# Combining the attention groups inside the attention stage, with five weight slots instead of seven

## The chip, the core and the metric

The kernel runs on one core of a Trainium2 chip as a single program. The metric is the device time of one execution in microseconds (us). TensorE is called PE in the profile, VectorE DVE, ScalarE ACT, GpSimd POOL, and SP is the engine that issues most DMA transfers. PEld is PE's loading of the stationary operand, which overlaps with its matmuls.

## The reference

One step of a hybrid decoder layer over 2048 prompt tokens (and eight sample tokens, which ride along) with a model width of 1024. One wide input projection feeds everything. Three attention groups with different dilations share eight head slots, and per position the groups of a slot are averaged with weights from their softmax denominators; a gate multiplies the average. Beside it runs an HGRN2 recurrence with eight heads. Cut to what matters here:

```
GROUPS = ((128, 1), (512, 4), (2048, 16))          # (window, dilation)
h = rms_norm(x, norm_w)
for g, (win, dil) in enumerate(GROUPS):
    q, k, v = three 512-wide column groups of h @ w_in
    o[g], lse[g] = dilated_attn_prompt(q, k, v, win, dil, slopes[g])
mix = softmax(stack(lse), axis=0)                  # over the three groups
att = einsum('gnth,gnthe->nthe', mix, stack(o))
att = att * silu(h @ w_in[:, attention gate])
hq, fl, hi, hgate = four 1024-wide column groups of h @ w_in
ho, s_new = hgrn2_chunked(silu(hq) * dk**-0.5, ...)
ho = rms_norm(ho, hg_norm_w) * silu(hgate)
merged = sigmoid(ga) * (att @ w_att_proj) + sigmoid(gb) * (ho @ w_hg_proj)
y = x + merged @ w_out
```

## The kernel before

The tokens are worked off in two halves of 1024 (p = 0 and p = 1). For each half the program goes through `att_stage(p)`, `cb_stage(p)` and `hg_stage(p)`, in that order, with the natural-layout projections and the merges between and behind them. In the profiled execution the first half's three stages lie at about 262 to 706, 706 to 816 and 816 to 1245 us, those of the second half at 1600 to 2085, 2085 to 2180 and 2180 to 2550 us.

Projections. `t_pair` projects h onto two 128-wide groups of columns of w_in at once, by a scheme of seven products in place of eight. The seven operands on the token side are A11, S1, S2, A12, S3, S4, A22 (sums of quarters of h, made once); the seven on the weight side are W0 to W6, made by `w_combos` from four loaded quarters (`wr`). Each operand is split into a high part and a low part, hh/hl for tokens and wh/wl for weights, so that three matmuls (L413 hh with wh, L415 hl with wh, L416 hh with wl) over four slices of the contraction, 12 in all, make one product. The weight split is one ScalarE instruction (L193, writes wh) and one VectorE instruction that needs its result (L194, writes wl). The products go into three PSUM banks pa, pb and pc; intermediate sums are copied to `cc` by ScalarE (L420), and results leave through evacuation functions (VectorE L456 adds a cc). In the first half a pair is done in two passes, one of 256 and one of 260 columns, so each of the seven weights is used twice; in the second half one pass of 512 uses each once. The number of wh/wl buffers is the first argument of `open_T`, the number of wr buffers the second.

Attention. For each of four slots j and three groups g, `att_proj` projects q and k with one pair, and `att_side` of the (j, g) before it computes scores (L568 and L585), exponentials (L590), transposes of the probabilities (L600) and the weighted sums (L614), and stores the result with its denominators to `natt[g][j]`. The side matmuls go between those of the pair.

Combination. `att_gates(j)` is a pair that makes the gates of slots j and j+1 and stores them to `gs_scr`. `combine(j, cs)` loads, for each block c of 512 tokens, the three groups' results into `na` and averages them on VectorE (L672 to L688, with one exponential on ScalarE, L676); `combine_T` transposes the average (L696), multiplies it by the gate and stores it. `merge_pair` makes the merge gates (its bank is read by the ScalarE sigmoid L707). All of it stands in `cb_stage`.

HGRN. `hg_stage` does eight heads, each with a pair for gates and, shared by neighbours, pairs for f and q; the chain of a head (L912 to L967 and a normalization, L938 to L993) runs on the side, from `kn`, the copy of the transposed keys, on (L925).

The order on each engine is set by a scheduler from the order of the code and priorities, and is fixed in the program: an instruction waits for those ahead of it on its engine, and its buffers for their last readers.

Of the kernel before, what the change touches and what calls it, by code (L numbers as in the profile page):

```python
# [10 lines left out]
F32 = mybir.dt.float32  # L11
# [7 lines left out]
P = 128  # L19
# [57 lines left out]
def body(ctx, tc, x_p, x_s, c128, c512, c2048, st_in, norm_w, w_in, w_ap, w_hp, w_out, hg_nw, lbl, fin_w,  # L77
# [7 lines left out]
    sto = nc.sync.dma_start  # L85
# [5 lines left out]
    def pool(name, bufs=1, space=None):  # L91
        if space == DRAM:
            return tc.tile_pool(name=name, bufs=bufs, space=space)
        kw = {} if space is None else {"space": space}
        return tc.tile_pool(name=name, bufs=bufs, reuse_waits="tile", **kw)
# [46 lines left out]
    def ps_side():  # L142
        return cur["x"].tile([P, 512], F32, name="px", tag="px")
# [242 lines left out]
    def open_T(slots, raws):  # L386
        tp["st"] = ExitStack()
        tp["p"] = tp["st"].enter_context(pool("wt"))
        tp["n"] = slots, raws
# [57 lines left out]
    def put(dst, ps, add, view=lambda x: x):  # L447
        if add is None:
            A.copy(out=dst, in_=view(ps))
        else:  # L450
            V.tensor_tensor(out=dst, in0=view(ps), in1=view(add), op=ALU.add)

    def val(ps, add):
        if add is None:
            return ps
        V.tensor_tensor(out=add, in0=ps, in1=add, op=ALU.add)  # L456
        return add

    def att_proj(at, p, j, g):
        dil = GROUPS[g][1]  # L460
        qT = at.tile([P, HALF], F32, name="qT", tag="qT", bufs=2)
        kT = at.tile([P, HALF * (1 + p)], F32, name="kT", tag="kT", bufs=2)
        q4 = qT.rearrange("p (b r i) -> p b r i", b=2, r=4)
        q16 = qT.rearrange("p (r i) -> p r i", r=16)
        k4 = kT.rearrange("p (b r i) -> p b r i", r=4, i=P)
        k16 = kT.rearrange("p (h r i) -> p h r i", r=16, i=64)
        if p == 1:
            n = (128, 512, 1024)[g]
            dma(kT[:, 0:n], kscr[g][j])

        def evac(is_k):
            def f(r, off, npr, ps, add):
                t0 = r * 512 + off
                if dil == 1:
                    s0 = t0 + (P if is_k and p else 0)
                    put((kT if is_k else qT)[:, s0:s0 + npr], ps, add)
                elif dil == 4:
                    i0, ni = off // 4, npr // 4
                    o = k4[:, r + p] if is_k else q4[:, r]
                    put(o[:, :, i0:i0 + ni], ps, add, lambda x: x.rearrange("p (i r) -> p r i", r=4))  # L480
                else:
                    i0, ni = t0 // 16, npr // 16
                    o = k16[:, p] if is_k else q16
                    put(o[:, :, i0:i0 + ni], ps, add, lambda x: x.rearrange("p (i r) -> p r i", r=16))
            return f

        c0 = g * 1536 + j * P
        t_pair(p, (c0, c0 + AW), (g * 8 + j, g * 8 + 4 + j), (evac(False), evac(True)))
        if p == 0:
            sto(kscr[g][j], (kT[:, HALF - P:HALF], kT[:, 512:1024], kT)[g])  # L490
        return qT, kT
# [156 lines left out]
            if n < 6:  # L648
                a, b = na, score(n + 3)

    def att_gates(pl, p, j, sto=sto):
        def evac(j):
            def f(r, off, npr, ps, add):
                z = val(ps, add)
                gt = pl.tile([P, 512], F32, name="gm", tag="gm", bufs=3)[:, 0:npr]
                A.activation(out=gt, in_=z, func=AF.Sigmoid)
                V.tensor_tensor(out=gt, in0=z, in1=gt, op=ALU.mult)
                t0 = p * HALF + r * 512 + off
                sto(gs_scr[j][:, t0:t0 + npr], gt)
            return f  # L660

        t_pair(p, (OFF_G + j * P, OFF_G + (j + 1) * P), (48 + j, 49 + j), (evac(j), evac(j + 1)))

    def combine(cb, j, cs):
        pend = []
        for c in cs:
            na = cb.tile([P, 3, 4, 132], F32, name="na", tag="na", bufs=4)
            for g in range(3):
                dma(na[:, g], natt[g][j][c * 512:(c + 1) * 512].rearrange("(i u) c -> i u c", u=4))
            mx = cb.tile([P, 4, 2], F32, name="mx", tag="mx", bufs=2)  # L670
            w3 = cb.tile([P, 3, 4, 2], F32, name="w3", tag="w3", bufs=2)
            V.tensor_tensor(out=mx, in0=na[:, 0, :, 128:130], in1=na[:, 1, :, 128:130], op=ALU.min)  # L672
            V.tensor_tensor(out=mx, in0=mx, in1=na[:, 2, :, 128:130], op=ALU.min)
            for g in range(3):
                V.tensor_tensor(out=w3[:, g], in0=mx, in1=na[:, g, :, 128:130], op=ALU.subtract)
            A.activation(out=w3, in_=w3, func=AF.Exp)  # L676
            wd = cb.tile([P, 3, 4, 2], F32, name="wd", tag="wd", bufs=2)
            V.tensor_tensor(out=wd, in0=w3, in1=na[:, :, :, 130:132], op=ALU.mult)
            V.tensor_tensor(out=mx, in0=wd[:, 0], in1=wd[:, 1], op=ALU.add)
            V.tensor_tensor(out=mx, in0=mx, in1=wd[:, 2], op=ALU.add)  # L680
            V.reciprocal(out=mx, in_=mx)
            for g in range(3):
                V.tensor_tensor(out=w3[:, g], in0=w3[:, g], in1=mx, op=ALU.mult)
                nv = na[:, g, :, 0:128].rearrange("p u (h e) -> p u h e", h=2)
                V.tensor_tensor(out=nv, in0=nv, in1=w3[:, g].unsqueeze(3).to_broadcast([P, 4, 2, E]), op=ALU.mult)
            nv = na[:, 0, :, 0:128]
            V.tensor_tensor(out=nv, in0=nv, in1=na[:, 1, :, 0:128], op=ALU.add)
            V.tensor_tensor(out=nv, in0=nv, in1=na[:, 2, :, 0:128], op=ALU.add)  # L688
            pend.append((c, na))
        return j, pend  # L690

    def combine_T(cb, j, pend):
        for c, na in pend:
            pt = ps_side()
            for u in range(4):
                TE.transpose(pt[:, u * P:(u + 1) * P], na[:, 0, u, 0:128], ident)  # L696
            gt = cb.tile([P, 512], F32, name="gc", tag="gm", bufs=3)
            dma(gt, gs_scr[j][:, c * 512:(c + 1) * 512])
            V.tensor_tensor(out=gt.rearrange("p (i u) -> p u i", u=4), in0=pt.rearrange("p (u i) -> p u i", u=4),
                            in1=gt.rearrange("p (i u) -> p u i", u=4), op=ALU.mult)  # L700
            sto(att_scr[j][:, c * 512:(c + 1) * 512], gt)

    def merge_evac(mp, p, a, d, sto=sto):
        def f(r, off, npr, ps, add):
            z = val(ps, add)
            gt = mp.tile([P, 512], F32, name="gm", tag="gm", bufs=3)[:, 0:npr]
            A.activation(out=gt, in_=z, func=AF.Sigmoid)  # L707
            t0 = p * HALF + r * 512 + off
            sto(g_scr[a][d][:, t0:t0 + npr], gt)
        return f  # L710

    def merge_cols(a, d):
        return (OFF_MA, OFF_MB)[a] + d * P

    def merge_pair(mp, p, d, W=None, sto=sto):
        t_pair(p, (merge_cols(1, d), merge_cols(1, d + 1)), (60 + d, 61 + d),
               (merge_evac(mp, p, 1, d, sto), merge_evac(mp, p, 1, d + 1, sto)), W)
# [111 lines left out]

    def cb_stage(p):  # L830
        with pool("cb") as cb:
            fill = [lambda j=j: att_gates(cb, p, j) for j in (0, 2)]
            fill += [lambda d=d: merge_pair(cb, p, d) for d in ((0, 2) if p == 0 else (2, 4))]
            for j in range(4):
                if fill:
                    fill.pop(0)()
                if j:
                    combine_T(cb, *pend)
                pend = combine(cb, j, (2 * p, 2 * p + 1))
            for f in fill:  # L840
                f()
            combine_T(cb, *pend)

    def hg_stage(p):
# [307 lines left out]
        return samp_hg_prep, samp_hg_calc, samp_hg_state, samp_hg_out, samp_hg_end  # L1152

    def att_stage(p):
        with pool("at") as at:
            pend = None
            for j in range(4):
                for g in range(3):
                    nxt = (p, j, g) + att_proj(at, p, j, g) if pend is None else None
                    if pend is not None:  # L1160
                        att_side(at, *pend)
                        nxt = (p, j, g) + att_proj(at, p, j, g)
                    pend = nxt
            att_side(at, *pend)

    alloc_H()
    with banks(6, ABC), pool("wn") as wn, right("px") as px:
# [58 lines left out]
        for u, (g, half) in enumerate(((1, 0), (2, 0), (3, 0), (3, 1))):  # L1226
            nat_block(wn, 0, g, half)
            cs = slice(u * P, (u + 1) * P)
# [11 lines left out]

    bk = banks(3, ABC)
    bk.__enter__()
    open_T(7, 5)
    att_stage(0)
    cb_stage(0)
    hg_stage(0)
# [243 lines left out]
```

## Time and profile before

| | |
|---|---|
| median of 3 runs | 3054.38 us (3054.3 to 3061.18) |
| profiled execution | 3056.5 us |
| its span in the profile | 3054.6 us |
| mean granted clock of PE | 0.979 |
| PE busy | 2884.6 us, 94% of the span |
| DVE, ACT busy | 1851.9 us (61%), 1468.7 us (48%) |

How to read the rows further down. The clock is a share of the full one. A table of windows gives, for each stretch (its bounds and its length in us), the busy time and count of instructions of PE, PEld, DVE, ACT and POOL, then PE's granted clock, the busy share of the DMA engines and the GB/s that they moved. A row of waits gives the waiting engine, tile and line, what it waited for, and then the total in us, the number of such waits and the longest. A timeline row gives the start and the duration in us, engine, line, operation, output<-inputs, shape, and in brackets the idle time of the engine before it with what ended it. A row on a tile gives the instructions with this tile as an operand: how many, then the shortest, median and longest duration in ns.

### The profile page before, as it was taken

The numbers are of one execution on the slowest core, as the hardware profiler recorded it, in microseconds if no ns is written. First come the engines' busy times: TensorE is split into PE (matmuls) and PEld (weight loads), VectorE is DVE, ScalarE is ACT, GpSimd is POOL, SyncE is SP. The second block draws the span as 40 slices with busy tenths as digits, with TensorE's granted clock in tenths as the row PEclk, the third lists the DMA queues.
The fourth block names the chain that finished last, engine by engine and source line by source line (L and its number), as shares of the span: only waits on it lengthen the run. The fifth ranks groups of instructions, "written<-read, shape, count | busy, mean of one in ns | idle before, by whom it ended". The sixth has DMA issues, their size and how long they took to land. (4 is left out here: it accounts for less than half of the span.)

```text
span 3054.6 us, 54166 instructions
## 1 busy us (share of the span) xinstructions
PE 2884.6 (94%) x20318; PEld 2502.7 (82%) x20318; DVE 1851.9 (61%) x4603; ACT 1468.7 (48%) x3271; POOL 2.5 (0%) x8
## 2 busy tenths in 40 slices
PE   8998999998899999989979999999999999999999
PEld 7997878888898999888866676777788887899886
DVE  7454455557777777666345555558877777544443
ACT  6333454545576676532334444445677773311232
POOL 0000000000000000000000000000000000000000
PEclk9999999999999999999989999999999999999999
DMA  5453222215421222457753222326322224744542
GB/s 188 141 173 112 70 60 82 82 57 173 129 64 60 76 64 83 162 173 242 206 149 87 83 86 79 93 64 205 93 81 73 78 76 151 224 135 136 161 150 78
DMA packets 453362, 357.45 MB, mean 117 GB/s; under 512 B 28505, under 2 KB 411818, under 8 KB 452178
## 3 DMA queue, kind: packets, MB, share of 16 engines
q1 hardware_dynamic: 452482, 351.93, 38.2%
q8 instruction: 162, 2.65, 0.4%
q0 software_dynamic: 320, 1.05, 0.1%
q14 instruction: 110, 0.90, 0.1%
q10 hardware_dynamic: 288, 0.92, 0.1%
HBM read 241.06 MB, written 113.26 MB: 116 GB/s over the span
## 5 line engine op out<-in xcount | busy, mean ns | idle before, releaser
L193 ACT ACTIVATE wh<-wr 128x512 fp32r<-128x512 f32 (+1 forms) x543 | 366.5, 681 | 523.1 <-PE pb L415 196.5
L194 DVE TENSOR_TENSOR wl<-wr,wh 128x512 fp32r<-128x512 f32 (+1 forms) x543 | 405.5, 752 | 240.9 <-ACT wh L193 213.4
L413 PE MATMUL pc<-hhS,wh 128*128 128x256 f32 (+2 forms) x816 | 266.3, 326 | 5.1 <-PEq L1348 3.9
L415 PE MATMUL pc<-hlS,wh 128*128 128x256 f32 (+2 forms) x816 | 264.7, 324 | 0.0
L416 PE MATMUL pc<-hhS,wl 128*128 128x256 f32 (+2 forms) x816 | 264.0, 324 | 0.0
L413 PE MATMUL pa<-hhA,wh 128*128 128x256 f32 (+2 forms) x612 | 204.7, 335 | 24.9 <-ACT gm L707 7.6
L590 ACT ACTIVATE sc<-sc,stg 128x256 f32<-128x256 f32 (+2 forms) x384 | 171.6, 448 | 99.8 <-DVE stg L588 96.5
L413 PE MATMUL pb<-hhA,wh 128*128 128x260 f32 (+2 forms) x612 | 203.9, 333 | 9.6 <-ACT wh L193 4.4
L415 PE MATMUL pa<-hlA,wh 128*128 128x256 f32 (+2 forms) x612 | 200.8, 328 | 0.0
L416 PE MATMUL pa<-hhA,wl 128*128 128x256 f32 (+2 forms) x612 | 200.6, 328 | 0.0
L415 PE MATMUL pb<-hlA,wh 128*128 128x260 f32 (+2 forms) x612 | 200.3, 327 | 0.0
L416 PE MATMUL pb<-hhA,wl 128*128 128x260 f32 (+2 forms) x612 | 198.9, 325 | 0.0
L588 DVE CUSTOM_DVE_ANT_0 sc<-px,bt 128x256 f32<-128x256 f32 (+2 forms) x384 | 123.6, 352 | 124.1 <-PE px L585 39.0
L413 PEld LDWEIGHTS pc<-hhS,wh 128*128 128x128 f32 x816 | 155.1, 190 | 19.4 <-issue 6.9
L193 ACT ACTIVATE th<-ra 128x256 fp32r<-128x256 f32 (+1 forms) x148 | 57.3, 417 | 224.9 <-PE pp L1399 157.4
L415 PEld LDWEIGHTS pc<-hlS,wh 128*128 128x128 f32 x816 | 155.1, 190 | 12.1 <-issue 1.5
L416 PEld LDWEIGHTS pc<-hhS,wl 128*128 128x128 f32 x816 | 155.1, 190 | 11.4 <-issue 0.2
L413 PEld LDWEIGHTS pa<-hhA,wh 128*128 128x128 f32 x612 | 117.6, 192 | 37.6 <-ACT gm L707 9.1
L600 PE MATMUL px<-cm,sc 128*128 128x128 f32 (+1 forms) x600 | 131.1, 294 | 17.0 <-ACT sc L590 15.2
L413 PE MATMUL pb<-hhS,wh 128*128 128x260 f32 (+1 forms) x408 | 136.2, 334 | 8.8 <-ACT cc L420 8.8
L413 PE MATMUL pa<-hhS,wh 128*128 128x256 f32 (+1 forms) x408 | 137.5, 337 | 7.5 <-ACT cc L420 7.5
L416 PE MATMUL pa<-hhS,wl 128*128 128x256 f32 (+1 forms) x408 | 135.9, 333 | 0.0
(476 smaller groups left out, 8319.3 us busy)
## 6 DMA issues: line engine op xcount, KB each, us to landing
wr<-in_w_in SPq DMA_DIRECT2D x272, 256.0 KB
wr<-in_w_in SPq DMA_DIRECT2D x40, 512.0 KB
vt<-vscr SPq DMA_DIRECT2D x52, 256.0 KB
na<-natt SPq DMA_DIRECT2D x48, 264.0 KB
vscr<-vst SPq DMA_DIRECT2D x48, 256.0 KB
natt<-stg SPq DMA_DIRECT2D x32, 264.0 KB
xt<-in_x_prompt SPq DMA_DIRECT2D x16, 512.0 KB
iscr<-vst SPq DMA_DIRECT2D x32, 256.0 KB
```

Source lines behind the costliest of these rows:

```text
L193: A.activation(out=hi, in_=raw, func=AF.Copy)
L194: V.tensor_tensor(out=lo, in0=raw, in1=hi.bitcast(F32), op=ALU.subtract)
L413: TE.matmul(o, wh[:, k], hi[:, k, off:off + n], start=(first and k == 0), stop=False, skip_group_check=True)
L415: TE.matmul(o, wh[:, k], lo[:, k, off:off + n], start=False, stop=False, skip_group_check=True)
L416: TE.matmul(o, wl[:, k], hi[:, k, off:off + n], start=False, stop=(k == 3), skip_group_check=True)
L588: V.tensor_tensor_reduce(out=sc[:, hx, 0:W], in0=spss[hx][:, 0:W], in1=bt[:, hx, BW - W:BW], scale=-0.125, scalar=3e38, op0=ALU.add, op1=A ...
L590: A.activation(out=sc[:, hx, 0:W], in_=sc[:, hx, 0:W], func=AF.Exp, scale=-1.0, bias=stg[:, u, 128 + hx:129 + hx], accum_out=stg[:, u, 130 ...
L600: TE.transpose(pt[0:kw, (hx * nw + w) * P:(hx * nw + w + 1) * P], sc[:, hx, w * kw:(w + 1) * kw], ident)
```

## The change

- `open_T(7, 5)` becomes `open_T(5, 5)` for the first half: five buffers each for wh and wl instead of seven, with seven weights a pair as before.
- `att_stage` now issues `att_gates` of slots 0 and 1 at its start and of slots 2 and 3 ahead of (j, g) = (2, 0).
- `combine` of slot j-1 is issued inside slot j, one block c at g = 1 and one at g = 2, and `combine_T` of that block one iteration of (j, g) later. Slots 0 to 2 go this way, six blocks in each half.
- `cb_stage` keeps two merge pairs, and `combine` and `combine_T` of slot 3.
- The buffers of `na` in the attention stage are two in the first half and one in the second, instead of four; the gate tiles share their three buffers with the scores (tag "sc").

```diff
-    def att_gates(pl, p, j, sto=sto):
+    def att_gates(pl, p, j, tag=("gm", 3)):
...
-    def combine(cb, j, cs):
+    def combine(cb, j, cs, nb=4):
         pend = []
         for c in cs:
-            na = cb.tile([P, 3, 4, 132], F32, name="na", tag="na", bufs=4)
+            na = cb.tile([P, 3, 4, 132], F32, name="na", tag="na", bufs=nb)
...
-    def combine_T(cb, j, pend):
+    def combine_T(cb, j, pend, tag=("gm", 3)):
...
     def cb_stage(p):
         with pool("cb") as cb:
-            fill = [lambda j=j: att_gates(cb, p, j) for j in (0, 2)]
-            fill += [lambda d=d: merge_pair(cb, p, d) for d in ((0, 2) if p == 0 else (2, 4))]
-            for j in range(4):
-                if fill:
-                    fill.pop(0)()
-                if j:
-                    combine_T(cb, *pend)
-                pend = combine(cb, j, (2 * p, 2 * p + 1))
-            for f in fill:
-                f()
+            merge_pair(cb, p, 2 * p)
+            pend = combine(cb, 3, (2 * p, 2 * p + 1))
+            merge_pair(cb, p, 2 * p + 2)
             combine_T(cb, *pend)
...
     def att_stage(p):
+        tag = ("sc", 3)
         with pool("at") as at:
-            pend = None
+            att_gates(at, p, 0, tag)
+            pend = done = None
             for j in range(4):
                 for g in range(3):
-                    nxt = (p, j, g) + att_proj(at, p, j, g) if pend is None else None
                     if pend is not None:
                         att_side(at, *pend)
-                        nxt = (p, j, g) + att_proj(at, p, j, g)
-                    pend = nxt
+                    if done is not None:
+                        combine_T(at, *done, tag)
+                        done = None
+                    if j and g:
+                        done = combine(at, j - 1, (2 * p + g - 1,), 2 - p)
+                    if (j, g) == (2, 0):
+                        att_gates(at, p, 2, tag)
+                    pend = (p, j, g) + att_proj(at, p, j, g)
             att_side(at, *pend)
+            combine_T(at, *done, tag)
...
-    open_T(7, 5)
+    open_T(5, 5)
```

What this does to the order on the engines is shown at two places. The first is the pair of (j, g) = (2, 2) in the first attention stage. On PE before, where the sixth product (S4, weight W5, its low part here wl_6475) and the seventh (A22, W6 = wh_6478) of the first pass end and the second pass begins with A11 and W0 (wh_6449):

```order
L416 MATMUL pc_6484<-hhS4_170,wl_6475 128x256
L413 MATMUL pa_6482<-hhA22_172,wh_6478 128x256
L415 MATMUL pa_6482<-hlA22_173,wh_6478 128x256
L416 MATMUL pa_6482<-hhA22_172,wl_6479 128x256
...
L413 MATMUL pb_6579<-hhA11_160,wh_6449 128x260
L415 MATMUL pb_6579<-hlA11_161,wh_6449 128x260
L416 MATMUL pb_6579<-hhA11_160,wl_6450 128x260
```

The first pass is finished before the second begins, and all seven weights stand ready. On PE in the changed kernel, at the same pair, from the end of the second pass's A11 product (weight W0 = wh_7114) on; W5 is wh_7139 and W6 wh_7143:

```order
L415 MATMUL pb_7244<-hlA11_161,wh_7114 128x260
L416 MATMUL pb_7244<-hhA11_160,wl_7115 128x260
L413 MATMUL pc_7149<-hhS4_170,wh_7139 128x256
L415 MATMUL pc_7149<-hlS4_171,wh_7139 128x256
L413 MATMUL pb_7244<-hhS2_164,wh_7126 128x260
...
L416 MATMUL pc_7149<-hhS4_170,wl_7140 128x256
...
L416 MATMUL pc_7246<-hhS1_162,wl_7122 128x260
L413 MATMUL pb_7244<-hhS2_164,wh_7126 128x260
L415 MATMUL pb_7244<-hlS2_165,wh_7126 128x260
L416 MATMUL pb_7244<-hhS2_164,wl_7127 128x260
L413 MATMUL pa_7147<-hhA22_172,wh_7143 128x256
```

S4 and A22 of the first pass now stand behind A11 and S1 of the second: W5 gets the buffer of W0, W6 that of W1, and each is split after the second use of the weight whose buffer it takes. Between A11 and S4 nothing is left, between the second and third matmul of S4 stand four of S2, and between S1 and A22 three of S2.

On ScalarE in the changed kernel at the same pair (wh_7578 is W0 of the next pair):

```order
L420 COPY cc_7190<-pa_7147 128x256
L193 ACTIVATE wh_7139<-wr_7112 128x512
L420 COPY cc_7259<-pb_7244 128x260
L193 ACTIVATE wh_7143<-wr_7108 128x512
L193 ACTIVATE wh_7578<-wr_7570 128x512
```

The splits of W5 and W6 stand directly around the copy of the second pass's A11 result, where before it was the splits for the next pair that stood there.

The second place is a gate pair of the first HGRN stage. On VectorE before, the end of a head's chain around the evacuation of bank pb (cc_11072):

```order
L963 SCALAR_TENSOR_TENSOR R_10948<-R_10930,eb_9829,us_10925 128x128
L456 TENSOR_TENSOR cc_11072<-pb_11058,cc_11072 128x256
L967 COPY ob_9831<-px_10945 128x128
L923 TENSOR_TENSOR am_10955<-px_10951,cm_149 128x128
L963 SCALAR_TENSOR_TENSOR R_10966<-R_10948,eb_9829,us_10943 128x128
```

Here the evacuation stands in the middle of the chain, with further chunks of the head (R, ob, am) still to come. In the changed kernel, where the lines of the chain have numbers lower by seven:

```order
L956 SCALAR_TENSOR_TENSOR R_11000<-R_10994,eb_9829,us_10989 128x128
L931 TENSOR_TENSOR sq_11003<-ob_9831 128x512
L960 COPY ob_9831<-px_10997 128x128
L932 TENSOR_REDUCE ss_10861<-sq_11003 128x4
L931 TENSOR_TENSOR sq_11006<-ob_9831 128x512
L456 TENSOR_TENSOR cc_11072<-pb_11058,cc_11072 128x256
```

The evacuation has moved behind the whole chain, its squares and its first reduction.

## Rows read from the trace of the kernel before

**Rows 1.** The page, busy time of each engine.

```profile
PE 2884.6 (94%) x20318; PEld 2502.7 (82%) x20318; DVE 1851.9 (61%) x4603; ACT 1468.7 (48%) x3271; POOL 2.5 (0%) x8
```

**Rows 2.** Windows by stage: attention, combination, HGRN; attention and combination of the second half.

```profile
262.00:706.00 444.00, 430.44 (x3688) 365.59 (x3689) 235.87 (x749) 214.99 (x654) 0.00 (x0) 0.98 0.26 76
706.00:816.00 110.00, 96.95 (x747) 94.95 (x746) 86.37 (x247) 56.80 (x108) 0.00 (x0) 0.94 0.56 175
...
850.00:1245.00 395.00, 370.35 (x3005) 362.18 (x3006) 303.17 (x842) 263.41 (x564) 0.00 (x0) 0.98 0.23 70
1600.00:2085.00 485.00, 472.42 (x2922) 337.35 (x2919) 266.60 (x725) 237.46 (x642) 0.00 (x0) 0.99 0.31 90
2085.00:2180.00 95.00, 85.33 (x357) 66.26 (x356) 76.71 (x187) 52.08 (x79) 0.00 (x0) 0.95 0.51 162
```

**Rows 3.** Waits of PE in the first attention stage, 262 to 706 us.

```profile
PE px L600 <- ACT sc L590: 9.2, 21, 1.5
```

**Rows 4.** Waits of PE in the first combination stage, 706 to 816 us.

```profile
PE pa L413 <- DVE cc L456: 6.2, 3, 2.6
PE pb L413 <- ACT cc L420: 3.0, 2, 2.3
```

**Rows 5.** Waits of PE in the first HGRN stage, 850 to 1245 us.

```profile
PE px L930 <- ACT kn L925: 17.4, 7, 2.5
PE pa L413 <- ACT gm L707: 5.8, 6, 1.0
```

**Rows 6.** Timeline of a split for the next pair, in the HGRN stage.

```profile
1011.92 0.28 PE L415 MATMUL pb<-hlA,wh 128*128 128x260 f32 x1
...
1012.04 0.28 PE L416 MATMUL pb<-hhA,wl 128*128 128x260 f32 x1
...
1012.16 0.28 PE L413 MATMUL pc<-hhS,wh 128*128 128x260 f32 x1
...
1012.24 0.63 ACT L193 ACTIVATE wh<-wr 128x512 fp32r<-128x512 f32 x1 [0.66 <-PE pb L415]
```

**Rows 7.** Timeline of the first split of the first attention stage.

```profile
262.61 0.63 ACT L193 ACTIVATE wh<-wr 128x512 fp32r<-128x512 f32 x1 [3.14 <-DMA wr<-in_w_in]
...
263.29 0.58 PE L413 MATMUL pa<-hhA,wh 128*128 128x256 f32 x1 [5.55 <-ACT wh L193]
...
264.02 0.28 PEld L416 LDWEIGHTS pa<-hhA,wl 128*128 128x128 f32 x1 [0.23 <-DVE wl L194]
```

**Rows 8.** Tile na in the first combination stage, 706 to 850 us.

```profile
L685 DVE TENSOR_TENSOR na<-na,w x24: 678/684/711, 726.1 to 792.9; 128x512 f32<-128x512 f32 x24
...
L688 DVE TENSOR_TENSOR na<-na x8: 678/683/715, 731.4 to 796.1; 128x512 f32<-128x512 f32 x8
```

**Rows 9.** Timeline of a head in the first HGRN stage.

```profile
1028.53 0.38 PE L930 MATMUL px<-vi,kn 128*128 128x128 f32 x1 [2.54 <-ACT kn L925]
...
1039.27 0.63 DVE L967 COPY ob<-px 128x128 f32<-128x128 f32 x2
...
1040.18 0.68 DVE L938 TENSOR_TENSOR sq<-ob 128x512 f32<-128x512 f32 x1
...
1041.12 0.68 DVE L939 TENSOR_REDUCE ss<-sq 128x4 f32<-128x512 f32 x1
...
1046.38 0.39 PE L413 MATMUL pa<-hhA,wh 128*128 128x260 f32 x1 [0.96 <-ACT gm L707]
```

**Rows 10.** Two windows of 6 us in the first attention stage.

```profile
326.00:332.00 6.00, 4.41 (x33) 3.20 (x32) 3.31 (x15) 2.57 (x12) 0.00 (x0) 0.95 0.33 92
332.00:338.00 6.00, 6.00 (x25) 3.83 (x24) 1.60 (x9) 2.31 (x10) 0.00 (x0) 0.50 0.00 0
```

More of the change, by code (lines that the diff above doesn't have):

```diff
@@ L654, in f @@
                 z = val(ps, add)
-                gt = pl.tile([P, 512], F32, name="gm", tag="gm", bufs=3)[:, 0:npr]
+                gt = pl.tile([P, 512], F32, name="gm", tag=tag[0], bufs=tag[1])[:, 0:npr]
                 A.activation(out=gt, in_=z, func=AF.Sigmoid)
@@ L662, in att_gates @@
         t_pair(p, (OFF_G + j * P, OFF_G + (j + 1) * P), (48 + j, 49 + j), (evac(j), evac(j + 1)))
-    def combine(cb, j, cs):
+    def combine(cb, j, cs, nb=4):
         pend = []
         for c in cs:
-            na = cb.tile([P, 3, 4, 132], F32, name="na", tag="na", bufs=4)
+            na = cb.tile([P, 3, 4, 132], F32, name="na", tag="na", bufs=nb)
             for g in range(3):
                 dma(na[:, g], natt[g][j][c * 512:(c + 1) * 512].rearrange("(i u) c -> i u c", u=4))
-            mx = cb.tile([P, 4, 2], F32, name="mx", tag="mx", bufs=2)
-            w3 = cb.tile([P, 3, 4, 2], F32, name="w3", tag="w3", bufs=2)
+            mx = cb.tile([P, 4, 2], F32, name="mx", tag="mx", bufs=min(nb, 2))
+            w3 = cb.tile([P, 3, 4, 2], F32, name="w3", tag="w3", bufs=min(nb, 2))
             V.tensor_tensor(out=mx, in0=na[:, 0, :, 128:130], in1=na[:, 1, :, 128:130], op=ALU.min)
@@ L676, in combine @@
             A.activation(out=w3, in_=w3, func=AF.Exp)
-            wd = cb.tile([P, 3, 4, 2], F32, name="wd", tag="wd", bufs=2)
+            wd = cb.tile([P, 3, 4, 2], F32, name="wd", tag="wd", bufs=min(nb, 2))
             V.tensor_tensor(out=wd, in0=w3, in1=na[:, :, :, 130:132], op=ALU.mult)
@@ L696, in combine_T @@
                 TE.transpose(pt[:, u * P:(u + 1) * P], na[:, 0, u, 0:128], ident)
-            gt = cb.tile([P, 512], F32, name="gc", tag="gm", bufs=3)
+            gt = cb.tile([P, 512], F32, name="gc", tag=tag[0], bufs=tag[1])
             dma(gt, gs_scr[j][:, c * 512:(c + 1) * 512])
```

## The prediction

> **What bounds the kernel now.** I read the page first: TensorE (PE) is busy 2884.6 of 3054.6 us, 94%, and VectorE 61%, ScalarE 48% [rows 1]. So what can change is the 170 us in which PE stands still, and the stretches in which its clock is low. Next I cut the span at the stages. In the first attention stage PE idles 13.6 of 444 us, in the first combination stage 13.05 of 110 at a clock of 0.94, in the HGRN stage behind it 24.65 of 395 at 0.98; in the second half 12.6 of 485 and 9.67 of 95 at 0.95 [rows 2]. The densest idle time is thus where the change takes work away (12% and 10%), and the thinnest where it puts work in (3%). Then the waits of each stretch: in the first attention stage 21 waits for the exponentials are 9.2 us of the 13.6 [rows 3]; in the first combination stage what ends PE's waits is the late emptying of a PSUM bank by VectorE or ScalarE, 6.2 us for three waits and 3.0 for two [rows 4]; in the HGRN stage seven waits for kn, the first copy of a head, are 17.4 us, and six for a bank that a gate still reads 5.8 [rows 5]. Nowhere in these lists does PE wait for a weight split in steady state: the splits run a pass ahead.
>
> **Part 1: seven weights in five slots.** This touches all 34 pairs of the first half, and I price it by one split. In a running pair the split of a next pair's weight starts on ScalarE at 1012.24, 0.32 us behind the issue of the L415 matmul that read the slot last (1011.92) and 0.20 behind that of the last matmul of the product (1012.04); PE meanwhile goes on to the next matmul at 1012.16, 0.12 later [rows 6]. It doesn't care, because the weight is for later. With five slots W5 takes the slot of W0 and is wanted as soon as W0's second use is over (second and third order lists above): the same release now stands between two neighbouring products. What PE then sees is shown once before, at the first pair of the stage: wh starts at 262.61, PE's first matmul at 263.29 (0.68 later), and the wl that the third matmul needs lets it go at 264.02 (1.41 later) [rows 7]. So, counted from the issue of the product's last matmul, wh is there at 0.20 + 0.68 = 0.88 and wl at 0.20 + 1.41 = 1.61. PE would have issued at 0.12: it loses 0.76. Its third matmul would come 0.24 behind the first, at 1.12: without something in between it loses another 0.49, 1.25 in all.
>
> What stands in between is read from the order, at each kind of pair.
> - Attention (12 pairs and the two of the gates). Behind W0's second use come two matmuls of S4, four of S2, the rest of S4: the wait for wl is covered, the 0.76 is not. For W6 three matmuls of S2 (0.36) stand between the release and A22, and nothing between A22's second and third: 0.88 - 0.12 - 0.36 + 0.49 = 0.89. Together 1.65, in 13 of 14 pairs (at the second gate pair scores and transposes lie between): **+21.5**.
> - The merge pairs and the first two HGRN projections around the combination: neither covered (2 x 1.25), both nearly (0.6), W5 not (1.3), nearly both (0.3): **+4.7**; the two merge pairs behind the HGRN stage 1.0 and 2.3: **+3.3**.
> - HGRN, eight gate pairs: S4 follows bare, 1.25; W6 has six matmuls of S2 ahead of it, nothing. In these pairs the VectorE order changes too (last two lists): the emptying of pb stands behind the whole chain of the head, so behind a copy (half of 0.63), a reduction (0.68) and a square (0.68) [rows 9], 1.67 us, of which PE's usual 0.32 for a release passes anyway: 1.35. Against it, PE waits 0.96 at the head of the next pair for the gate before the split [rows 9]; a PE that comes later finds most of that gone, 0.7. So 8 x (1.25 + 1.35 - 0.7) = 15.2; six f/q pairs, which have four side matmuls as cover, 0.35 each: 2.1. **+17.3**. The 2.54 us wait for kn [rows 9] stays: its chain on ScalarE is untouched.
>
> Sum of the part: 46.8 us. From both sides: nothing, if each falls on time PE would have idled (rival 4); 34 x 2.5 = 85 if no cover worked. I take the value that the order gives, being the only one that counts cover pair by pair. The gate on the clock: in the HGRN stage 24.65 us of idle go with 0.02 x 395 = 7.9 us of clock [rows 2], 0.3 per us; on its 17.3 new us that is **+5**. In the attention stage 13.6 us go with a similar share, but its new gaps are 0.8 us between full products, and I charge nothing (rival 3 does).
>
> **Part 2: six blocks of combination and the gates in the first attention stage.** A block is 3 x 0.684 + 2 x 0.683 = 3.4 us of large VectorE work [rows 8] and some 1.8 of small, 5.2; six are 31 us for an engine that is busy 236 of 444 us [rows 2]. They can only delay the scores' subtraction behind which the exponentials stand. The trace has no such mix. Bounds: nothing, and what a block costs in the combination stage, (13.05 + 6.6) / 8 = 2.46 with 0.06 x 110 = 6.6 of clock. VectorE is at half load, nearer to nothing: 0.5 each, **+3**. The gate pairs and the transposes only change place on PE. So do the loads and stores of the blocks and gates: they come into a stretch with a DMA share of 0.26 [rows 2], hidden; if not, they would delay wr, whose loads stand in the same queue and run a pair ahead. ScalarE loads fewer tables in all, since Sigmoid and Exp alternate less; no term.
>
> **Part 3: the combination stage of the first half.** Two of eight blocks, and no gates, stay. What it loses to idle and clock, 19.65, goes by three quarters: **-14.7**. Bounds: nothing (the same banks wait behind merge gates), and all of it. The next 34 us up to the first heads stay as they are.
>
> **Part 4: the second half.** It keeps its weight slots and its one pass. The same gain from 9.67 + 0.05 x 95 = 14.4, three quarters: -10.8. But there a single na buffer holds the block: loads of the next wait for the transposes an iteration later, and the copy of stg and the score buffers stand behind; 1.0 a block for six (same bounds): **-4.8** net.
>
> **Sum.** 46.8 + 5 + 3 - 14.7 - 4.8 = +35.3. The profiled execution took 3056.5, so 3091.8; it stood 2.1 above the median of the three runs, so **3090 us**, and by the bounds above 3070 to 3110 for this case.
>
> **Rivals.**
> 1. *The HGRN stage gives time back.* In the f/q pair three chunks of the head's chain now stand earlier on PE. If that starts kn early enough, the 2.54 of a head and the 0.96 of its gate vanish, 8 x 3.5 = 28, and the split waits there fall under them: instead of +17.3 and +5 there are -28, so 3090 - 50 = 3040. It decides from 2.8 of these 3.5 a head. Against it: kn waits for ScalarE's table loads and exponentials, which stand as before. 0.12.
> 2. *Combination blocks cost as much among the scores as before*, 2.46 each: 6 x (2.46 - 0.5) = +11.8 in the first attention stage, 6 x (14.4 / 8 - 1.0) = +5 in the second: 3107. For it: the waits for exponentials that are there already are the largest [rows 3]. 0.11.
> 3. *The clock follows the small gaps.* One stretch with PE busy 4.41 of 6 us was followed by 6 us at 0.50 [rows 10]. If the 29.5 us of new waits outside the HGRN stage cost half as much again: +15, 3105. For it the low clock just there; against it that the gaps of part 1 are shorter, with full products on either side. 0.10. The Trainium skill, "TensorE: Matmul & The Clock Gate", section "A second HAM failure mode: psum-queue depth-cycling", says that tiny idles between groups of matmuls can make the clock swing though PE looks busy. By that rule this rival would be the forecast; the HGRN stage, whose short waits stand at 0.98, bears it out only in part.
> 4. *No difference*: the split waits fall on time in which PE would wait for exponentials (9.2) and kn (17.4) anyway, which leaves 46.8 - 26.6 = 20.2 of part 1 and the 3 of part 2 against 19.5 of gain: 3060 in the profiled execution, 3058. Against it: of the 34 pairs most have no such wait at the place. 0.10.
>
> **How the numbers follow.** The forecast has 0.57. By over 0.3% (9 us, about what three runs can tell from no change here) faster is below 3045, slower above 3063.5. Faster: rival 1 and a little of rival 4, 0.13; same: the rest of it and the forecast's low edge, 0.11; slower: the rest, 0.76. The range goes from 3048, which leaves out rival 1, to 3112, above rivals 2 and 3.
>
> **What would show it.** Right: in the first 1300 us waits of PE L413 for wh L193 and of L416 for wl L194, tens of them at 0.4 to 0.9 us, some 21 us in the attention stage; a head of the HGRN stage about 2 us longer; combination stages with 3 and 4 us of idle instead of 13 and 10. Wrong: no such waits, or waits for exponentials that shrink by as much, or a clock in the first attention stage below 0.96.

## The result and the profile after

The changed kernel takes 3092.0 us (median of four runs, 3090.33 to 3095.81) against 3054.34 us before, a ratio of 1.0119 with a 95% interval of 1.0105 to 1.0133: slower by 37.7 us, where 35.3 was the forecast of the sum and 3090 the forecast of the time. The profiled execution took 3090.33 us with a span of 3088.6.

The page after, span and busy time of the engines:

```profile
span 3088.6 us, 54129 instructions
PE 2903.0 (94%) x20318; PEld 2502.0 (81%) x20318; DVE 1853.6 (60%) x4603; ACT 1463.8 (47%) x3266; POOL 2.5 (0%) x8
```

The same 20318 matmuls are now 18.4 us longer "busy" than in [rows 1], at a clock that is no lower (0.983 against 0.979). So about half of the loss doesn't show as idle time of PE at all; the section on the hardware says why.

To see where the time went I cut both traces at the same work: every pair of the first half has 168 matmuls of L413, L415 and L416, so the starts of number 18 x 168, 32 x 168 and 34 x 168 bound the attention and combination with the first two HGRN projections (18 pairs), fourteen HGRN pairs, the two merge pairs behind them, and all the rest. The windows between these marks, of the changed kernel (columns as in [rows 2]):

```profile
263.50:870.80 607.30, 572.58 (x4688) 491.21 (x4689) 346.22 (x1063) 298.88 (x819) 0.00 (x0) 0.99 0.31 91
870.80:1285.00 414.20, 377.15 (x2956) 360.11 (x2955) 299.22 (x831) 257.70 (x550) 0.00 (x0) 0.98 0.22 66
1285.00:1338.40 53.40, 45.63 (x345) 43.00 (x345) 29.85 (x50) 26.49 (x45) 0.00 (x0) 0.97 0.62 211
1338.40:3088.60 1750.20, 1663.76 (x10301) 1379.31 (x10299) 1032.96 (x2428) 764.33 (x1650) 2.29 (x4) 0.98 0.43 127
```

and of the kernel before:

```profile
263.30:858.60 595.30, 561.77 (x4680) 494.06 (x4680) 348.65 (x1064) 303.17 (x822) 0.00 (x0) 0.97 0.31 93
858.60:1248.10 389.50, 365.15 (x2964) 356.97 (x2964) 299.90 (x833) 257.86 (x551) 0.00 (x0) 0.98 0.24 70
1248.10:1300.60 52.50, 45.19 (x347) 43.17 (x346) 30.80 (x46) 27.27 (x47) 0.00 (x0) 0.97 0.59 211
1300.60:3054.60 1754.00, 1668.79 (x10301) 1380.40 (x10299) 1027.36 (x2428) 764.18 (x1648) 2.29 (x4) 0.98 0.43 126
```

| stretch | change in length | forecast, from the terms of the sum |
|---|---|---|
| 18 pairs: attention, combination | +12.0 | 21.5 + 4.7 + 3 - 14.7 = +14.5 |
| 14 HGRN pairs | +24.7 | 17.3 + 5 = +22.3 |
| two merge pairs | +0.9 | +3.3 |
| all the rest, with the second half | -3.8 | -4.8 |

These are single executions. Where two traces have the same code in the first 18 pairs, their lengths differ by some 4 us: 595.3 and 599.2 with the first half as before, 585.5 and 589.6 in the two runs with seven slots below. The HGRN pairs differ less: 388.3 to 393.9 us in eight traces with seven or six slots, 414.1 to 414.7 in three with five and no other edit there.

The waits of PE in the first attention stage after, which answer to [rows 3]:

```profile
PE pc L413 <- ACT wh L193: 9.6, 15, 1.5
PE pa L413 <- ACT wh L193: 7.4, 10, 5.3
PE px L600 <- ACT sc L590: 2.9, 8, 0.7
...
PE pa L416 <- DVE wl L194: 2.0, 9, 0.2
```

Of 25 waits for wh the two longest, 5.3 and 1.5 us, belong to the stage's first splits; both places had a wait before (5.55, [rows 7], and 1.0). The other 23, and the nine for wl, are new. One of them in the timeline, at a pair of slot 1:

```profile
452.71 0.28 PE L416 MATMUL pb<-hhA,wl 128*128 128x260 f32 x1
452.91 0.63 ACT L193 ACTIVATE wh<-wr 128x512 fp32r<-128x512 f32 x1 [3.77 <-PE pb L415]
...
453.59 0.38 PE L413 MATMUL pc<-hhS,wh 128*128 128x256 f32 x1 [0.60 <-ACT wh L193]
```

From the last matmul of A11 (452.71) to the split's start are 0.20 us, to PE's next issue 0.88: the two numbers that the prediction had taken from a place where PE did not wait ([rows 6]) and from the head of the stage ([rows 7]). In the whole stage this interval is 0.88 twelve times and 0.93 once, that before A22 is 0.52 nine times.

The waits of the HGRN stage after, which answer to [rows 5], and the place of the two new ones:

```profile
PE px L923 <- ACT kn L918: 17.0, 7, 2.6
PE pb L413 <- DVE cc L456: 11.3, 7, 1.7
PE pc L413 <- ACT wh L193: 4.4, 8, 0.6
PE pc L416 <- DVE wl L194: 1.6, 7, 0.2
```

```profile
1003.71 0.28 PE L416 MATMUL pa<-hhS,wl 128*128 128x256 f32 x1
1003.82 0.28 DVE L960 COPY ob<-px 128x128 f32<-128x128 f32 x1
1004.02 0.68 DVE L932 TENSOR_REDUCE ss<-sq 128x4 f32<-128x512 f32 x1
1004.62 0.68 DVE L931 TENSOR_TENSOR sq<-ob 128x512 f32<-128x512 f32 x1
1005.21 0.42 DVE L456 TENSOR_TENSOR cc<-pb,cc 128x256 f32<-128x256 f32 x1
...
1005.69 0.39 PE L413 MATMUL pb<-hhA,wh 128*128 128x260 f32 x1 [1.70 <-DVE cc L456]
...
1007.12 0.28 PE L416 MATMUL pb<-hhA,wl 128*128 128x260 f32 x1
1007.32 0.63 ACT L193 ACTIVATE wh<-wr 128x512 fp32r<-128x512 f32 x1 [1.24 <-PE pb L415]
...
1008.00 0.38 PE L413 MATMUL pc<-hhS,wh 128*128 128x256 f32 x1 [0.60 <-ACT wh L193]
...
1008.73 0.38 PE L416 MATMUL pc<-hhS,wl 128*128 128x256 f32 x1 [0.23 <-DVE wl L194]
```

PE has nothing left but the second pass's A11, whose bank pb is emptied only behind a copy, a reduction and a square of the head: 1005.69 - 1003.71 - 0.12 = 1.86 us lost. Behind it the bare split of W5 costs 1008.00 - 1007.12 - 0.12 = 0.76, and its wl 0.38 (1008.73 - 1008.23 - 0.12, where 1008.23 is the issue of the L415 matmul ahead of it).

### The profile page after: what moved, and what is told of

Read it like the earlier page. It is cut to its first block, busy times and chain, and to the rows that moved or that the text cites. A ratio compares the mean times of both kernels' runs of the same rounds, so it can differ in the third digit from the quotient of the medians.

```text
span 3088.6 us, 54129 instructions
## 1 busy us (share of the span) xinstructions
PE 2903.0 (94%) x20318; PEld 2502.0 (81%) x20318; DVE 1853.6 (60%) x4603; ACT 1463.8 (47%) x3266; POOL 2.5 (0%) x8
## 5 line engine op out<-in xcount | busy, mean ns | idle before, releaser
L413 PE MATMUL pc<-hhS,wh 128*128 128x256 f32 (+2 forms) x816 | 272.4, 334 | 27.7 <-ACT wh L193 16.6
L416 PE MATMUL pc<-hhS,wl 128*128 128x256 f32 (+2 forms) x816 | 265.2, 325 | 2.9 <-DVE wl L194 2.6
L415 PE MATMUL pc<-hlS,wh 128*128 128x256 f32 (+2 forms) x816 | 264.7, 324 | 0.0
L413 PE MATMUL pb<-hhA,wh 128*128 128x260 f32 (+2 forms) x612 | 203.4, 332 | 22.0 <-DVE cc L456 12.4
L413 PE MATMUL pa<-hhA,wh 128*128 128x256 f32 (+2 forms) x612 | 207.8, 340 | 12.6 <-ACT wh L193 8.9
L416 PE MATMUL pa<-hhA,wl 128*128 128x256 f32 (+2 forms) x612 | 202.1, 330 | 3.0 <-DVE wl L194 3.0
L415 PE MATMUL pb<-hlA,wh 128*128 128x260 f32 (+2 forms) x612 | 198.8, 325 | 0.0
L415 PE MATMUL pa<-hlA,wh 128*128 128x256 f32 (+2 forms) x612 | 198.2, 324 | 0.0
L416 PE MATMUL pb<-hhA,wl 128*128 128x260 f32 (+2 forms) x612 | 198.1, 324 | 0.0
L413 PEld LDWEIGHTS pc<-hhS,wh 128*128 128x128 f32 x816 | 154.2, 189 | 54.1 <-ACT wh L193 23.8
L416 PEld LDWEIGHTS pc<-hhS,wl 128*128 128x128 f32 x816 | 154.5, 189 | 17.5 <-DVE wl L194 4.8
L415 PEld LDWEIGHTS pc<-hlS,wh 128*128 128x128 f32 x816 | 154.5, 189 | 12.0 <-issue 0.9
L413 PEld LDWEIGHTS pb<-hhA,wh 128*128 128x128 f32 x612 | 116.4, 190 | 35.9 <-DVE cc L456 14.0
L413 PE MATMUL pa<-hhS,wh 128*128 128x256 f32 (+1 forms) x408 | 135.5, 332 | 9.2 <-ACT cc L420 9.2
L413 PEld LDWEIGHTS pa<-hhA,wh 128*128 128x128 f32 x612 | 116.0, 189 | 32.6 <-ACT wh L193 11.6
L600 PE MATMUL px<-cm,sc 128*128 128x128 f32 (+1 forms) x600 | 129.6, 292 | 11.4 <-ACT sc L590 9.3
L413 PE MATMUL pb<-hhS,wh 128*128 128x260 f32 (+1 forms) x408 | 134.0, 328 | 0.4 <-ACT cc L420 0.4
```

The source lines that it names most:

```text
L413: TE.matmul(o, wh[:, k], hi[:, k, off:off + n], start=(first and k == 0), stop=False, skip_group_check=True)
L415: TE.matmul(o, wh[:, k], lo[:, k, off:off + n], start=False, stop=False, skip_group_check=True)
L416: TE.matmul(o, wl[:, k], hi[:, k, off:off + n], start=False, stop=(k == 3), skip_group_check=True)
L600: TE.transpose(pt[0:kw, (hx * nw + w) * P:(hx * nw + w + 1) * P], sc[:, hx, w * kw:(w + 1) * kw], ident)
```

## Experiments

The theory is that of the prediction, called here the theory of the slots: the loss is the splits of W5 and W6 that PE waits for and the late emptying of pb, all of it in the first half; moving the combination gains, by less. The main rival is the placement: combination blocks and gates among the scores cost the time, and the slots are hidden. Each run was timed beside the kernel before, which stood between 3054 and 3061 in these comparisons, so the ratios are what to compare.

**Five slots alone.**

```diff
-    open_T(7, 5)
+    open_T(5, 5)
```

in the kernel before, first half. 

> The kernel before with open_T(5, 5) in the first half and nothing else. Theory of the slots (the loss is the splits of W5 and W6 that PE now waits for, and the later emptying of pb in the HGRN gate pairs): the changed kernel stands 37.7 above before although the second half gave 3.8 and the shorter combination stage some 11.7 net, so the slots alone are worth 53: 3107, between 3095 and 3112, with the waits for wh L193 in both stages. Rival, the placement (the combination blocks and gates among the scores cost the time, the slots are hidden): within 9 us of before, 3046 to 3063.

Ratio 1.0169 (1.0141 to 1.0197), 3112.19 us: 52 us above before, where 53 was expected. Its waits from the attention stage to the first heads (264 to 885 us):

```profile
PE pc L413 <- ACT wh L193: 13.1, 18, 2.5
PE pa L413 <- ACT wh L193: 8.3, 11, 5.3
PE pb L413 <- DVE cc L456: 6.3, 3, 2.6
```

The waits for wh are those of the changed kernel, without any move of the combination. The placement falls, since the slots are not hidden; they cost more than the whole loss, and the rest of the change gives about 52 - 37.7 = 14 back, with some 10 us of scatter either way from the two intervals.

**Seven slots.** The changed kernel with

```diff
-                        done = combine(at, j - 1, (2 * p + g - 1,), 2 - p)
+                        done = combine(at, j - 1, (2 * p + g - 1,), 1)
...
-    open_T(5, 5)
+    open_T(7, 5)
```

> The changed kernel with open_T(7, 5) in the first half, and one na buffer instead of two in the attention stage of the first half (seven slots leave no room for two). Theory of the slots: waits for wh L193 and the late emptying of pb disappear, what is left is the gain, 3054 - 3.8 - 11.7 = 3039, up to 3 more for the single na buffer: 3039 to 3045, faster than both. Rival, the placement: the time stays above 3080, and the waits in the attention stage are for L600 and for banks that wait behind combination work on VectorE.

Ratio 0.9949 (0.9936 to 0.9963), in a second run 0.9969 (0.9955 to 0.9983). The HGRN pairs are back at 391.5 us, the first 18 pairs take 585.5, which is 9.8 less than before. The attention stage has no waits in steady state for wh any more, but a new kind:

```profile
PE pa L413 <- DVE qT L451: 8.5, 3, 2.8
PE px L600 <- ACT sc L590: 6.8, 17, 0.9
PE pa L413 <- ACT wh L193: 5.5, 1, 5.5
```

**One na buffer, five slots.** The first line of that edit alone. 

> The changed kernel with one na buffer instead of two in the first half, and five slots as they are. The runs with seven slots also had one buffer; this one tells whether that edit was worth something by itself. If not: 3092 within 5 us. If the single buffer costs what the second half was charged for it in the prediction (1.0 a block, six blocks): 3095 to 3100. If it helps, seven slots explain less than the run with them showed.

Ratio 1.0121 (1.0092 to 1.0149): no difference from the changed kernel. So the run with seven slots owes its time to the slots.

**Six slots**, one na buffer: `open_T(6, 5)`. 

> The changed kernel with six weight slots in the first half and one na buffer. Only W6 has to wait for a slot, that of W0, and six matmuls of S1 (0.72 us) stand between the second A11 and A22, with nine more S1 around it. By the step of the prediction (0.88 - 0.12 less what stands between) its price is near nothing: 3041 to 3050, as with seven slots. Rival: each weight that is used in both passes and has to share a slot costs the same, whatever stands between, so one of two weights half the loss: 3065 to 3075.

Ratio 0.9964 (0.9951 to 0.9977): as seven slots. A slot that is used twice costs nothing that these runs can tell where the split has cover; the loss is not one price for each weight that shares.

**Seven slots from the HGRN stage on.** The changed kernel with

```diff
     cb_stage(0)
+    close_T()
+    open_T(7, 5)
     hg_stage(0)
```

> The changed kernel, but the weight buffers are closed and opened again with seven slots ahead of the first HGRN stage; attention and combination keep five. Theory of the slots: the pairs from the HGRN stage on lose their 24.7 us against before (and 1 of the merges), 3092 - 25 = 3067, with 1 to 3 us for the reopening; a pair of heads falls from 57.2 to 53.8 us at full clock. Rival, the placement: 3092, since nothing of the attention stage changes. Rival, a third cause in the HGRN stage that does not hang on the slots (the heads come in another state of the clock or of the queues): the heads stay at 57.

Ratio 1.0057 (1.0033 to 1.0081), that is 0.6% or 19 us below the changed kernel, less than was expected. The heads did what they should: the fourteen HGRN pairs take 388.7 us, as before the change (389.5) and not 414.2. What is missing went into the reopening itself, between 756 and 827 us:

```profile
PE pa L413 <- ACT wh L193: 12.6, 2, 12.0
```

PE stands for 12.0 us, not the 1 to 3 that I had put down. The split that it waits for is itself waiting for a load:

```profile
825.86 0.63 ACT L193 ACTIVATE wh<-wr 128x512 fp32r<-128x512 f32 x1 [10.80 <-DMA wr<-in_w_in]
```

The buffers of wr are closed and opened with those of wh and wl, so the next pair's loads no longer run a pair ahead. SP issues them at 821.32, behind the last stores of the combination (820.00), 7 us after PE's last matmul (814.5).

**Early emptying of pb.** The changed kernel; `merge_evac` of the HGRN stage gives its addition priority:

```diff
-            z = val(ps, add)
+            if early:
+                with tc.high_priority(HP):
+                    z = val(ps, add)
+            else:
+                z = val(ps, add)
...
-                (merge_evac(hp, p, 0, h), evac))
+                (merge_evac(hp, p, 0, h, early=p == 0), evac))
```

> The changed kernel, in which the emptying of pb by the merge gate in the HGRN gate pairs of the first half has priority, so that it stands ahead of the head's chain on VectorE and the second pass's A11 goes between the side matmuls on PE, with S3 between it and S4. If the late emptying (1.86 us a pair in the trace of the changed kernel) and the bare split of W5 behind it (0.76, and 0.38 for wl) are what a head pays, seven to eight of them fall away: 3092 - 15 to - 24, 3068 to 3077, a pair of heads back at 54 to 55 us. Rival: a head is bound by its chain on ScalarE and VectorE, and what is taken from the bank's wait comes back as a wait for kn or at the next gate: 3088 to 3092.

Ratio 1.0079 (1.0053 to 1.0105): 12 us below the changed kernel, under what was expected. Its waits in the HGRN stage:

```profile
PE px L927 <- ACT kn L922: 18.0, 13, 2.6
PE pc L413 <- ACT wh L193: 4.4, 8, 0.6
PE pa L413 <- ACT gm L711: 2.8, 6, 0.5
```

The wait for the bank (11.3 us) is gone, and the fourteen HGRN pairs take 400.6 us, 13.6 less than in the changed kernel. The split of W5 is still bare in seven of the eight waits for wh (0.88 from issue to issue): S3 did not come between as I had read from the order at one place. Counted from issue to issue the bank gave 12.4 us, and about a third of that came back at the next gate (0.75 instead of 0.38, six times) and ahead of kn (six new waits, each an interval of 0.45). Both theories had a part of it: the late emptying is a cost of its own, but this edit did not get all of it back.

**The second half alone.** The first half as before, the second as in the changed kernel. 

> First half as before (seven slots, combination in its own stage), second half as in the changed kernel. Theory of the slots: the second half alone gives the 3.8 us that the traces show from 1300.6 and 1338.4 us on, 3050 to 3051. Rival: the single na buffer of the second half costs as much as the shorter combination stage gives and the 3.8 is scatter of the clock: 3054 to 3057.

Ratio 0.9980 (0.9963 to 0.9997): 6 us faster, with an interval from 1 to 11. The 3.8 of the traces lies in it, and the second half is not what makes the kernel slower. From the end of the first half's pairs on, the nine traces with this second half take 1745.7 to 1754.4 us (mean 1751.0) and the two with the old one 1754.0 and 1758.7, so the exact gain is not settled.

**Gates among the scores, blocks in the combination stage.** Seven slots; `cb_stage(0)` does all four slots j of `combine` with its two merge pairs, and `att_stage(0)` has no `combine`. 

> Seven slots; in the first half only the two gate pairs stand in the attention stage, and all eight combination blocks stay in the combination stage with its two merge pairs; second half as in the changed kernel. If the gain of the first half comes from taking the blocks off the stage where PE waits for them, it is lost here, and eight blocks of 5.2 us of VectorE beside two pairs of 19.7 us make the stage worse: 3050 to 3065. If it came from the gates as filler among the scores, the time is that of seven slots with the blocks moved: 3040 to 3046.

Ratio 1.0021 (1.0008 to 1.0033): 0.5 to 0.7% worse than the two runs of the same kernel with the blocks moved. The waits of its combination (725 to 869 us):

```profile
PE px L696 <- DVE na L688: 11.0, 5, 3.5
PE pa L413 <- ACT kt L856: 7.6, 2, 6.8
```

Without the gate pairs as cover PE waits for the blocks themselves: moving the gates alone does not bring the gain of the first half. Moving the blocks alone was not run. Its attention stage tells what a block costs among the scores: 14 pairs take 461.7 us without blocks and 479.0 with six of them (seven slots), 2.9 us each; 482.4 in the second run of that kernel would make it 3.4.

**The block behind the pair.** From the seven-slot kernel; what a block's 2.9 us are is seen in its timeline of VectorE and PE:

```profile
490.03 0.28 PE L416 MATMUL pc<-hhS,wl 128*128 128x260 f32 x1
...
490.54 0.69 DVE L687 TENSOR_TENSOR na<-na 128x512 f32<-128x512 f32 x1
491.14 0.69 DVE L194 TENSOR_TENSOR wl<-wr,wh 128x512 fp32r<-128x512 f32 x1
491.74 0.69 DVE L688 TENSOR_TENSOR na<-na 128x512 f32<-128x512 f32 x1
...
492.42 0.57 DVE L451 TENSOR_TENSOR qT<-pa,cc 128x256 f32<-128x256 f32 x1
...
493.13 0.36 PE L413 MATMUL pa<-hhA,wh 128*128 128x256 f32 x1 [2.83 <-DVE qT L451]
```

The block's products, alternating with splits, stand ahead of the emptying of pa. The three such waits (8.5 us) are half of what the six blocks cost (17.3). Another part is the clock: directly behind each of them PE runs some 3.4 us at the half level (1.2 GHz), here

```profile
493.40:496.80 3.40, 3.40 (x18) 3.40 (x17) 0.73 (x3) 0.06 (x1) 0.00 (x0) 0.50 0.64 227
```

where matmuls are issued every 0.21 us instead of 0.12; that would be some 1.5 us behind each wait, an estimate. The edit issues the block behind the pair, in both halves:

```diff
-                    if j and g:
-                        done = combine(at, j - 1, (2 * p + g - 1,), 1)
                     if (j, g) == (2, 0):
                         att_gates(at, p, 2, tag)
                     pend = (p, j, g) + att_proj(at, p, j, g)
+                    if j and g:
+                        done = combine(at, j - 1, (2 * p + g - 1,), 1)
```

> Seven slots and one na buffer, and the combination block of an iteration is issued behind its attention pair instead of ahead of it. In the trace of the seven-slot run three emptyings of a bank (qT, L451) stand on VectorE behind a block's products and the splits between them, and PE waits 2.8 us for each, 8.5 in all. If these waits are what a block costs among the scores, they go: 8 us less than the seven-slot kernel, about 3036 where that is 3044, ratio to before 0.992. Rival: the block's work then delays the scores' subtraction or the next pair's splits by as much: the same time as the seven-slot kernel.

> The seven-slot kernel with one na buffer once more, on the same chip as the run with the later block, for a comparison of the two: ratio to before 0.995 as in its first run, and the three waits for qT L451 of 2.8 us.

Ratio 0.9923 (0.9908 to 0.9939) against 0.9969 (0.9955 to 0.9983) for the seven-slot kernel on the same chip: 0.5%, 14 us, with 8 expected; the attention stage of 14 pairs falls to 469.8 us, which leaves 1.4 us for a block. What is left of those waits:

```profile
PE px L600 <- ACT sc L590: 9.3, 21, 1.5
...
PE pa L413 <- DVE qT L451: 1.5, 3, 0.7
```

Seven us of the waits for qT are gone, but the waits for the exponentials have grown from 6.8 to 9.3, so the rival had a part. What I had not expected is the clock. The first 18 pairs, with seven slots and the block ahead of the pair, then behind it:

```profile
262.80:848.30 585.50, 557.37 (x4680) 490.47 (x4680) 348.32 (x1064) 296.49 (x816) 0.00 (x0) 0.98 0.33 94
264.20:838.30 574.10, 550.01 (x4679) 482.80 (x4680) 348.55 (x1063) 296.04 (x815) 0.00 (x0) 0.99 0.33 96
```

Of the 11.4 us between them PE's idle time gives 4.0 and the busy time of the same matmuls 7.4: after the stage's first pair there is no stretch at the half level left. This version, seven slots with the block behind the pair, beats both kernels of the case: 3034.71 us.

## Why the prediction was right, step by step

- *The price of one bare split.* 0.88 from issue to issue, 0.76 lost, was measured to the hundredth, and so was the 0.52 before A22 (0.40 lost). The wl wait was 0.38 and not 0.49, because the first matmul after a wait holds the next one back by 0.22 instead of 0.12, so part of it passes anyway.
- *Attention, +21.5.* Twelve waits of 0.76, one of 0.81, nine of 0.40 and nine for wl of 0.38 are 17.0; with 0.10 behind each of the 31, 20.1. W6 had more cover in some pairs than I had counted. With five slots the waits for the exponentials fell from 9.2 us to 2.9, so rival 4 holds for 6 us of it. Net, the first twelve pairs take 442.5 us with five slots alone, against 424.6 and 428.6 in the two traces of that code with seven: 14 to 18 us, where 12 x 1.65 = 19.8 were forecast.
- *HGRN, +17.3 and +5 for the clock: +24.7.* The sum was near, its parts less so. The emptying cost 1.86 (1.23 at the first head), not 1.35: I had let PE pass 0.32 and it can't, since it has nothing else to issue; the other 0.19 I can't place. The gate's wait at the next pair fell by 0.95 (from an interval of 1.33 to 0.38), not 0.7. Of the 2.1 for the f/q pairs the waits show at most 0.6. The clock of this stage stayed at 0.98, so the term of 5 us for it was wrong. Counted from issue to issue, seven emptyings, seven bare splits and seven waits for wl, less six gate waits, come to 14.7 of the 24.7 us; the other 10 are the longer intervals behind the waits and short waits for which the sum had no term, the clearest six of 0.47 us for the copy cc (L420). That the 5 stood for them was luck. Rival 1 falls: the waits for kn are 17.0 against 17.4.
- *The two merge pairs behind it, +3.3.* They measured +0.9; no run says why.
- *Moving the combination, 3 - 14.7 = -11.7.* With seven slots it measured -9.8 over the first 18 pairs; with five 607.3 against 621.1 for the slots alone, -13.8. But a block costs 2.9 us among the scores where the splits don't wait, not 0.5, above the bound (2.46) that rival 2 was made of; so the combination stage and the stretch behind it must have given some 27 (9.8 + 17.3) and not 14.7. Two terms were off in opposite directions, and that their sum came out was luck. What a block costs in the changed kernel itself, where the splits' waits cover some of it, no run separates. One place where more was given is "the next 34 us up to the first heads", which the prediction left as they are. Here are the two pairs ahead of the heads, before and after, and then all 18 pairs with five slots alone (the changed kernel has 607.30 us there, 572.58 of them busy):

```profile
802.20:858.60 56.40, 47.04 (x355) 45.98 (x352) 33.50 (x82) 33.76 (x65) 0.00 (x0) 0.91 0.28 88
817.10:870.80 53.70, 46.24 (x362) 43.73 (x361) 32.30 (x84) 34.85 (x68) 0.00 (x0) 1.00 0.26 78
264.30:885.40 621.10, 582.08 (x4689) 498.04 (x4689) 345.82 (x1063) 303.79 (x821) 0.00 (x0) 0.97 0.30 89
```

  The two pairs are at full clock after the change and shorter, though they now pay for bare splits. Of the 13.8 us that the move gives with five slots, 9.5 are busy time of the same matmuls at a higher granted clock, and 4.3 are idle time.
- *The second half, -4.8.* -3.8 in the traces, -6 in the run by itself: right within the scatter.
- *The clock, rival 3.* In the stretch of the first 18 pairs the clock is 0.99 after and was 0.97 before, with over 30 new short waits in it. The one stretch at the half level that it has behind its first splits comes at 547 us, behind a wait of 2.1 us for a bank, and none stands behind the short waits. So rival 3 falls. The Trainium skill, "TensorE: Matmul & The Clock Gate", section "A second HAM failure mode: psum-queue depth-cycling", tells of a kernel in which frequent micro-idles between groups of matmuls made the clock swing. Waits of 0.4 to 0.9 us between full products did not do so here.

## What to carry to other kernels

A buffer that is reused inside a unit of work turns a prefetch into a wait of the whole refill chain: release, write, semaphore, read (here 0.88 us for 0.12), unless other work for the engine stands between; count, at every place, the instructions between the last reader of the old content and the first of the new. Six buffers with that cover were as good as seven, five without it cost 52 us. And vector work that is moved beside a bottleneck has a price that its busy share doesn't tell: it is set by what stands right behind it on its engine, and issuing it after the work that frees a bank was worth 14 us. A wait of 2 to 3 us can cost more than itself: here a stretch at half clock stood behind many of them and behind none of the new waits under 1 us in the attention stage.

## What was not expected of the hardware

Idle time in the profile understates a wait of PE, here by some 0.26 us. At the pair of 452.71 us the issue was late by 0.76 and the row says 0.60, because the matmul ahead is drawn 0.28 long while matmuls are issued every 0.12; and the first matmul after the wait is drawn 0.38 long and lets the next issue after 0.22. This can account for PE's being 18.4 us "busier" with the same matmuls: in the first half there are some 85 more idle gaps than before, which at 0.26 make 22 us, an estimate, against 23.2 us more busy time in its three windows above. Where a kernel gains many short waits, the interval from issue to issue is the measure.
